# First stage of a two-layer trunk step: shift and scale from stationary weights, with the first query and key products made inside the stage

## The chip, the cores and the metric

The kernel runs on one core of a Trainium2 chip. A core has five engines that work side by side and meet through semaphores: TensorE (PE in the profile; its weight loads are listed as PEld), VectorE (DVE), ScalarE (ACT), GpSimd (POOL) and SyncE (SP). SP, ACT and POOL can issue DMAs, which run on 16 shared DMA engines. The metric is the time of one execution on the device in microseconds (us), the median of several runs.

## The reference

The reference is one inference step through two layers. 640 tokens of width 1024 go through it: 512 latent tokens on a grid and 128 context tokens. Layer 0 is neighbourhood attention with 16 heads, layer 1 a recurrent unit; after each comes a SwiGLU block. What matters here is the very beginning: the first normalization with its shift and scale, and the first query and key products.

```python
def _adaln(cond, w_mod, b_mod):
    m = jax.nn.silu(cond) @ w_mod + b_mod
    return jnp.split(m, N_MOD, axis=-1)

def _modulate(x, g, shift, scale):
    return _rms_norm(x, g) * (1 + scale[:, None, :]) + shift[:, None, :]

sh1_c, sc1_c, ... = _adaln(c_ctx[None, :], w_mod[i], b_mod[i])
sh1_l, sc1_l, ... = _adaln(c, w_mod[i], b_mod[i])
xm_c = _modulate(ctx, norm_g[i, 0], sh1_c, sc1_c)
xm_l = _modulate(lat, norm_g[i, 0], sh1_l, sc1_l)
q, k, v = jnp.split(xm @ w_qkv, 3, axis=-1)
```

There are two conditioning vectors (latent and context), so the shift and the scale of the first sub-layer are a product of a 2x1024 matrix with a 1024x2048 weight: 8 MB of weights for two rows of result.

## The kernel before

Activations lie with features on the 128 partitions and tokens along the free dimension: x is 8 feature tiles of 128x640. Every large product is made in three parts. Weights and activations are split into a high part of a reduced type (fp32r) and the rest, and hi x hi, hi x lo and lo x hi are added up in PSUM. The three products are lines 221, 222 and 223 (method `some`), for two chunks of 320 tokens each. One unit of 128 output features is thus 8 feature tiles x 3 products x 2 chunks = 48 products. `unit` (line 163) loads a unit's weights into `raw`, copies them to `whi` on ACT (line 180) and subtracts to get `wlo` on DVE (line 182); each of the three tags has 3 buffers.

The first stage is `start` (line 296). It works in this order:

1. The eight tiles of x are loaded on SP; each is squared on ACT and added to `ssq` on DVE (lines 315 to 319).
2. The shift and scale products come in four rounds of two feature tiles. The conditioning vectors, padded to 32 columns (`csp`), are the stationary side, and 256 columns of w_mod move (line 342). Four of the eight input tiles sit side by side in the array, so each result arrives in four parts on four groups of 32 partitions. The w_mod pieces come in 16 DMAs of 512 KB into 10 buffers (`sw`, `wb`).
3. The results are copied out of PSUM to a row (lines 353 and 354). A second product with a selection matrix `sel` adds the four parts and turns them so that features lie on partitions (line 357). Lines 363 and 364 make A (scale) and B (shift).
4. In the first round, `stat` turns the sum of squares into 1/rms for all tokens, spread over all partitions (lines 396 to 413, copied by line 347). POOL multiplies the odd feature tiles of x with it (line 350).
5. `scaled` applies A and B of the round before: the even tiles through `modulate` (lines 418 to 420), the odd ones on ACT (line 325) and `split` (lines 1076 and 1077). The results are the tiles `hi` and `lo` that all Q, K and V products read.

After `start`, `qk` (line 529) makes Q and K of the first head pair, 48 products each, `vq` the V columns of four heads (lines 236 to 238), and the loop over eight head pairs runs `attend(p)` and `qk(p + 1)`. The products of one pair fill PE while the softmax of another runs on DVE and ACT. `fill` puts one step of the other modulations (one POOL DMA `mraw` and two DVE products, line 250) behind a softmax.

The order of the instructions on each engine is mostly the planner's: it takes them in the order of the code, but lets later ones go first where an earlier one would wait by its own estimate. `tc.issue_after(ins)` pins an instruction behind another. That is why in the trace the first Q products stand between the shift and scale products.

[...] Buffers of a tag are taken in turn; `bufs` is their number.

## Time and profile before

| | |
|---|---|
| median of 3 runs | 1532.3 us (1531.98 to 1537.51) |
| span of the profiled execution | 1532.6 us |
| PE busy | 1483.2 us (97%) |
| DVE busy | 1062.8 us (69%) |
| ACT busy | 695.8 us (45%) |
| POOL busy | 256.1 us (17%) |
| bytes moved by DMA | 196.65 MB, 128 GB/s on average |
| first product of w_mod (line 342) | starts at 12.83 us |
| first Q product (line 221) | starts at 28.84 us |
| first V product (line 236) | starts at 57.64 us |

The profile is one execution on the chip. Its own time is the span, 0.3 us above the median. A timeline row reads: start and length in us, engine, line and operation, output <- inputs, shapes, count; in brackets the idle time before it and what ended it. A row with a count covers all instructions from the first start to the last end. A row of stretches reads: from:to, length, busy time of PE, weight loads, DVE, ACT and POOL with counts, then the clock granted to TensorE (1.00 is full), the share of time that the DMA engines are busy, and GB/s. Busy times of PE include pipelined ends, so the distance between the starts of two neighbouring rows is the cost of a product, not its length.

### The profile page before, as it was taken

What the parts mean: (1) busy time and instruction counts of PE and PEld (TensorE: products, weight loads), DVE (VectorE), ACT (ScalarE), POOL (GpSimd) and SP (SyncE); (2) the same over time, 40 slices, a digit from 0 to 9 for tenths busy, and PEclk for the clock granted to TensorE, in tenths of its full rate; (3) what the DMA queues carried; (4) which work ended last, traced back from release to release, by engine and by line L of the source; (5) the groups of instructions that cost most, each with busy time, mean ns of one, the idle gap of its engine ahead of it and who ended that gap; (6) DMA issues with size and microseconds to landing.
All of it is one profiled execution on the core that took longest, in us unless ns stands there. A gap on an engine that the chain in (4) does not pass through costs nothing.

```text
span 1532.6 us, 25990 instructions
## 1 busy us (share of the span) xinstructions
PE 1483.2 (97%) x10309; PEld 1438.5 (94%) x10309; DVE 1062.8 (69%) x2000; ACT 695.8 (45%) x1266; POOL 256.1 (17%) x270
## 2 busy tenths in 40 slices
PE   5999999989999999999999999999899999999997
PEld 4899999879999999999999988799899999999996
DVE  5668888969899888434443869885965656566556
ACT  5566767755333113312331478863534342424242
POOL 2101122100111110000000113230412323222210
PEclk8999999999999999999999999999999999999999
DMA  9545656445566664222223443334332231323221
GB/s 375 155 115 166 185 158 179 147 141 184 177 194 191 192 201 140 73 83 71 76 61 99 153 127 107 107 104 162 113 119 70 83 110 56 99 67 97 70 56 69
DMA packets 73098, 196.65 MB, mean 128 GB/s; under 512 B 8048, under 2 KB 25616, under 8 KB 72848
## 3 DMA queue, kind: packets, MB, share of 16 engines
q1 hardware_dynamic: 58832, 144.48, 30.0%
q0 software_dynamic: 13856, 50.35, 10.8%
q8 instruction: 81, 1.33, 0.4%
q14 instruction: 41, 0.34, 0.1%
q10 hardware_dynamic: 288, 0.16, 0.0%
HBM read 179.48 MB, written 8.92 MB: 123 GB/s over the span
## 4 chain that ended last, share of the span: by engine, by line
PE 85%; DVE 7%; ACT 4%; DMA 2%; issue 2%; SPq 0%; POOL 0%; POOLq 0%; DVEq 0%; ACTq 0%
PE mm L222 14%; PE mm L223 14%; PE mm L221 14%; PE mx L221 5%; PE mx L223 5%; PE mx L222 5%; PE mx L850 3%; PE mx L849 3%; PE mx L851 3%; PE op L687 2%; PE gp L1035 2%; PE tp L611 2%; PE mc L849 1%; PE mc L850 1%; PE mc L851 1%
## 5 line engine op out<-in xcount | busy, mean ns | idle before, releaser
L222 PE MATMUL mm<-big,whi 128*128 128x320 f32 (+3 forms) x1270 | 397.9, 314 | 3.0 <-DVE big L1077 2.1
L221 PE MATMUL mm<-big,whi 128*128 128x320 f32 (+3 forms) x1270 | 394.5, 313 | 3.7 <-ACT big L1076 2.3
L223 PE MATMUL mm<-big,wlo 128*128 128x320 f32 (+3 forms) x1270 | 396.8, 313 | 1.0 <-DVE wlo L182 1.0
L222 PEld LDWEIGHTS mm<-big,whi 128*128 128x128 f32 x1270 | 241.9, 190 | 6.6 <-DVE big L1077 4.4
L221 PEld LDWEIGHTS mm<-big,whi 128*128 128x128 f32 x1270 | 240.3, 190 | 7.5 <-ACT big L1076 2.8
L223 PEld LDWEIGHTS mm<-big,wlo 128*128 128x128 f32 x1270 | 241.5, 190 | 2.5 <-DVE wlo L182 1.4
L250 DVE SCALAR_TENSOR_TENSOR mprod<-mraw,csb 128x1024 f32<-128x1024 f32 x160 | 195.4, 1221 | 11.2 <-DMA mraw<-in_wm 10.7
L443 DVE SCALAR_TENSOR_TENSOR x<-mm,G,x 128x128 f32<-128x128 f32 (+3 forms) x205 | 83.5, 436 | 86.6 <-PE mm L223 86.6
L182 DVE TENSOR_TENSOR wlo<-raw,whi 128x1024 fp32r<-128x1024 f32 (+1 forms) x90 | 110.1, 1224 | 37.4 <-ACT whi L180 22.1
L180 ACT CAST whi<-raw 128x1024 fp32r<-128x1024 f32 (+1 forms) x74 | 76.8, 1037 | 110.1 <-PE mm L222 71.7
L221 PE MATMUL mm<-big,whx 128*128 128x320 f32 (+3 forms) x363 | 113.7, 313 | 0.0
L223 PE MATMUL mm<-big,wlx 128*128 128x320 f32 (+3 forms) x363 | 113.3, 312 | 0.0
L222 PE MATMUL mm<-big,whx 128*128 128x320 f32 (+3 forms) x363 | 113.1, 312 | 0.0
L246 POOL DMA_DIRECT2D mraw<-in_wm x80 | 43.3, 542 | 381.1 <-DVE mprod L250 264.9
L221 PE MATMUL mx<-big,whi 128*128 128x320 f32 (+3 forms) x298 | 93.5, 314 | 0.4 <-ACT big L1076 0.4
L223 PE MATMUL mx<-big,wlo 128*128 128x320 f32 (+3 forms) x298 | 93.0, 312 | 0.0
L222 PE MATMUL mx<-big,whi 128*128 128x320 f32 (+3 forms) x298 | 92.9, 312 | 0.0
L180 ACT CAST whx<-raw 128x1024 fp32r<-128x1024 f32 (+1 forms) x40 | 41.0, 1027 | 93.4 <-PE mm L222 54.2
L221 PE MATMUL mx<-big,whx 128*128 128x320 f32 (+3 forms) x245 | 75.6, 309 | 0.0
L223 PE MATMUL mx<-big,wlx 128*128 128x320 f32 (+3 forms) x245 | 75.5, 308 | 0.0
L1076 ACT CAST whi<-raw 128x1024 fp32r<-128x1024 f32 (+1 forms) x41 | 41.3, 1008 | 74.8 <-PE mm L222 45.0
L222 PE MATMUL mx<-big,whx 128*128 128x320 f32 (+3 forms) x245 | 75.2, 307 | 0.0
(301 smaller groups left out, 3620.8 us busy)
## 6 DMA issues: line engine op xcount, KB each, us to landing
raw<-in_gu SPq DMA_DIRECT2D x88, 512.0 KB, 3.6
mraw<-in_wm POOLq DMA_DIRECT2D x80, 512.0 KB, 4.0
raw<-in_dn SPq DMA_DIRECT2D x24, 512.0 KB, 3.7
raw<-in_wqk SPq DMA_DIRECT2D x16, 512.0 KB, 4.4
raw<-in_wi SPq DMA_DIRECT2D x16, 512.0 KB, 3.6
whi<-in_wi POOLq DMA_DIRECT2D x16, 512.0 KB, 4.0
raw<-in_dn SPq DMA_DIRECT2D x16, 448.0 KB, 3.4
sw<-in_wm SPq DMA_DIRECT2D x10, 512.0 KB, 10.5
```

The source lines that it names most:

```text
L180: nc.scalar.copy(hi, raw)
L182: nc.vector.tensor_tensor(lo, raw, hi.bitcast(F32), ALU.subtract)
L221: nc.tensor.matmul(ps, hi[:, k], xhi[:, k, s], start=(k == 0), stop=False)
L222: nc.tensor.matmul(ps, hi[:, k], xlo[:, k, s], start=False, stop=False)
L223: nc.tensor.matmul(ps, lo[:, k], xhi[:, k, s], start=False, stop=(k == last))
L246: nc.gpsimd.dma_start(w, self.i["wm"][l * 6 + j - 2, f])
L250: nc.vector.scalar_tensor_tensor(prod, w, 1.0, self.csb[:, s], ALU.mult, ALU.mult, accum_out=out[:, s, f:f + 1])
L443: self.nc.vector.scalar_tensor_tensor(xs, ps[:, a - t0:b - t0], G[:, s, f:f + 1], xs, ALU.mult, ALU.add)
L849: nc.tensor.matmul(ps, hi[:, k], xh[:, k], start=start and k == 0, stop=False, skip_group_check=not start)
L850: nc.tensor.matmul(ps, hi[:, k], xl[:, k], start=False, stop=False, skip_group_check=not start)
L851: nc.tensor.matmul(ps, lo[:, k], xh[:, k], start=False, stop=(k == KH - 1), skip_group_check=not start)
L1076: self.nc.scalar.copy(hi, v)
```

## The change

- **w_mod** is laid out anew: 16 pieces of 512 KB, one for each feature tile k and each of shift (j = 0) and scale (j = 1). Each piece has its own buffer (`sw{k}{j}`). Requests on SP stand in a fixed order: x, pieces of tile 0, weights of the first Q, pieces of tile 1, weights of the first K and second Q, then the pieces of tiles 2 to 7.
- **vectors(k)**: w_mod is now the stationary side. For each j and each of the 8 input tiles c, a 128x128 block of the piece is loaded and multiplied with the two conditioning columns. A and B come straight from PSUM (`coefficients`); the copies, the selection product and the products on POOL are gone.
- **Scaling**: x is multiplied with 1/rms on DVE (`normed`), ACT writes the high part (`high`), DVE the scaled x and the low part (`low`).
- **Products**: Q of pair 0, K of pair 0 and Q of pair 1 are made inside `start`, in six PSUM banks that stay open, feature tile by feature tile. The vectors of tile k + 1 stand ahead of the products of tile k. Their evictions are split off from `qk` (`queries`, `keys_tile`).
- **Order**: `order` pins every PE, DVE and ACT instruction of the stage behind the one before it on its engine.
- **Dummy products**: before the sum of squares is ready, PE multiplies the identity with itself six times and with each arriving tile of x.
- **Around it**: tag `r` has 2 buffers, K moves to the main pool, the activation of the spread conditioning vectors is pinned behind the last Q eviction, the DMA scratch is set to 4096.

```diff
-        "wm0": wm[0, :, :2 * D].reshape(2, 4, P, 2, 4, 256).transpose(3, 4, 0, 2, 1, 5),
+        "wm0": wm[0, :, :2 * D].reshape(KT, P, 2, KT, P).transpose(3, 2, 1, 0, 4),
...
     def start(self, hi, lo, sp, big):
         nc = self.nc
         b1 = self.t([P, KT], F32, "b1", 1, sp)
         nc.vector.tensor_scalar(b1, self.col("bsc"), 1.0, None, ALU.add)
         idle = big.rearrange("p k t -> p (k t)")
+        cond = self.cs.rearrange("p (s k) -> p k s", s=2)
+        last = {}
+
+        def order(engine, step, after=None):
+            with ExitStack() as st:
+                for ins in (last.get(engine), after):
+                    if ins is not None:
+                        st.enter_context(self.tc.issue_after(ins))
+                last[engine] = step().ins
+            return last[engine]
+
+        def pe(*args, **kw):
+            return order("PE", lambda: nc.tensor.matmul(*args, **kw))
+
+        def dve(op, *args, **kw):
+            return order("DVE", lambda: op(*args, **kw))
+
+        def act(*args, **kw):
+            return order("ACT", lambda: nc.scalar.activation(*args, **kw))
+
+        for k in range(KT):
             nc.sync.dma_start(self.x[:, k], self.i["x"][k * P:k * P + P])
+        pieces, us = {}, []
+
+        def request(k):
+            for j in range(2):
+                pieces[k, j] = self.t([P, KT, P], F32, f"sw{k}{j}", 1, sp)
+                nc.sync.dma_start(pieces[k, j], self.i["wm0"][k, j])
+
+        def weights(f):
+            raw, whi_, wlo_ = [self.t([P, KT, P], dt, v, 3) for dt, v in ((F32, "raw"), (F32R, "whi"), (F32R, "wlo"))]
+            nc.sync.dma_start(raw, self.i["wqk"][f])
+            us.append((whi_, wlo_, raw))
+        request(0)
+        weights(0)
+        request(1)
+        weights(KT)
+        weights(1)
+        for k in range(2, KT):
+            request(k)
+
+        aux = self.ps("at")
+        for _ in range(6):
+            pe(aux[:, 0:P], self.ident, self.ident, start=True, stop=True)
+        self.ssq = self.t([P, NTOK], F32, "ssq", 2, sp)
+        for k in range(KT):
+            pe(aux[:, 0:256], self.ident, self.x[:, k, 0:256], start=True, stop=True)
+            q = self.ssq if k == 0 else idle[:, 2048 + k % 4 * NTOK:2688 + k % 4 * NTOK]
+            act(q, self.x[:, k], AF.Square)
+            if k:
+                dve(nc.vector.tensor_tensor, self.ssq, self.ssq, q, ALU.add)
+
+        def vectors(k):
+            pm = self.ps("ss")
+            for j in range(2):
+                for c in range(KT):
+                    pe(pm[:, 2 * j:2 * j + 2], pieces[k, j][:, c], cond[:, c], start=(c == 0), stop=(c == KT - 1))
+            return pm
+
+        def coefficients(k, pm):
+            B, A = [self.t([P, 2], F32, v, 3, sp) for v in ("b0", "a0")]
+            dve(nc.vector.tensor_scalar, A, pm[:, 2:4], b1[:, k:k + 1], self.col("ng00", k), ALU.add, ALU.mult)
+            dve(nc.vector.tensor_scalar, B, pm[:, 0:2], self.col("bsh", k), None, ALU.add)
+            return A, B
+
+        blocks = range(0, NTOK, P)
+        for j, b in enumerate(blocks):
+            pe(aux[:, 256 + j:257 + j], self.ssq[:, b:b + P], self.ones[:, 0:1], start=True, stop=True)
+        v = self.t([P, 8], F32, "var", 2)[:, 0:NT]
+        dve(nc.vector.tensor_scalar, v, aux[:, 256:256 + NT], 1.0 / D, EPS, ALU.mult, ALU.add)
+        rs = self.t([P, 8], F32, "rs", 2)[:, 0:NT]
+        nc.gpsimd.tensor_tensor(rs, v, self.mhalf.broadcast_to([P, NT]), ALU.pow)
+        dg = self.t([P, NT, P], F32, "dg", 1, sp)
+        dve(nc.vector.tensor_tensor, dg, self.ident.unsqueeze(1).broadcast_to([P, NT, P]), rs.unsqueeze(2).broadcast_to([P, NT, P]), ALU.mult)
+        pm = vectors(0)
+        rr = [self.ps("kk") for _ in range(2)]
+        for j, b in enumerate(blocks):
+            pe(rr[j // 4][:, b % NLAT:b % NLAT + P], self.ones, dg[:, j], start=True, stop=True)
+
+        def whi(j):
+            hi_, lo_, raw = us[j]
+            act(hi_, raw, AF.Copy)
+
+        def wlo(j):
+            hi_, lo_, raw = us[j]
+            dve(nc.vector.tensor_tensor, lo_, raw, hi_.bitcast(F32), ALU.subtract)
+
+        def normed(k):
             for s, a, b in _pieces(0, NTOK):
                 v = self.x[:, k, a:b]
+                dve(nc.vector.tensor_tensor, v, v, r[:, a:b] if k else rr[s][:, 0:b - a], ALU.mult)
+
+        def high(k, A, B):
+            for s, a, b in _pieces(0, NTOK):
+                act(hi[:, k, a:b], self.x[:, k, a:b], AF.Identity, scale=A[:, s:s + 1], bias=B[:, s:s + 1])
+
+        def low(k, A, B):
+            for s, a, b in _pieces(0, NTOK):
+                v = self.x[:, k, a:b]
+                dve(nc.vector.tensor_scalar, v, v, A[:, s:s + 1], B[:, s:s + 1], ALU.mult, ALU.add)
+            dve(nc.vector.tensor_tensor, lo[:, k, 0:NTOK], self.x[:, k, 0:NTOK], hi[:, k, 0:NTOK].bitcast(F32), ALU.subtract)
+
+        def products(k, kind, tiles=range(3)):
+            for j in tiles:
+                w, m = us[j][kind == "lh"], (lo if kind == "hl" else hi)
+                for c, (t0, t1) in enumerate(CH):
+                    pe(pss[2 * j + c], w[:, k], m[:, k, t0:t1], start=(kind == "hh" and k == 0), stop=(kind == "lh" and k == KT - 1))
+
+        r = self.t([P, NTOK], F32, "ssq", 2, sp)
+        AB = {0: coefficients(0, pm)}
+        normed(0)
+        whi(0)
+        high(0, *AB[0])
+        for j, (_, t0, t1) in enumerate(_pieces(0, NTOK)):
+            act(r[:, t0:t1], rr[j][:, 0:t1 - t0], AF.Copy)
+        pss = [self.pg(False)[:, 0:HT]]
+        pss += [self.ps("kk")[:, 0:HT]]
+        low(0, *AB[0])
+        normed(1)
+        products(0, "hh", (0,))
+        pm = vectors(1)
+        products(0, "hl", (0,))
+        wlo(0)
+        AB[1] = coefficients(1, pm)
+        whi(1)
+        high(1, *AB[1])
+        whi(2)
+        low(1, *AB[1])
+        pss += [(self.ps("kk") if j % 2 else self.pg(False))[:, 0:HT] for j in range(4)]
+        products(0, "hh", (1,))
+        products(0, "hl", (1,))
+        products(0, "lh", (0,))
+        products(1, "hh", (0, 1))
+        products(0, "hh", (2,))
+        products(0, "hl", (2,))
+        products(1, "hh", (2,))
+        products(1, "hl")
+        wlo(1)
+        wlo(2)
+        normed(2)
+        pm = vectors(2)
+        products(0, "lh", (1, 2))
+        products(1, "lh")
+        AB[2] = coefficients(2, pm)
+        high(2, *AB[2])
+        low(2, *AB[2])
+        for k in range(2, KT):
+            if k + 1 < KT:
+                normed(k + 1)
+                pm = vectors(k + 1)
+                AB[k + 1] = coefficients(k + 1, pm)
+                high(k + 1, *AB[k + 1])
+                low(k + 1, *AB[k + 1])
+            for kind in ("hh", "hl", "lh"):
+                products(k, kind)
+        made = [self.queries(), self.keys_tile(), self.queries()]
+        for j in range(6):
+            t0, t1 = CH[j % 2]
+            made[j // 2][1](t0, slice(t0, t1), pss[j])
+        return [m[0] for m in made]
...
-    def qk(self, p, hi, lo, ap):
-        nc = self.nc
-        Q = self.t([P, NTOK], F32, "r", 1)
+    def queries(self):
+        nc = self.nc
+        Q = self.t([P, NTOK], F32, "r", 2)
...
-                nc.scalar.mul(Q[:, NLAT:NTOK], ps[:, 192:320], 0.125)
+                self.opened = nc.scalar.mul(Q[:, NLAT:NTOK], ps[:, 192:320], 0.125).ins
+        return Q, eq
+
+    def keys_tile(self):
+        nc = self.nc
+        K = self.t([P, 960], F32, "K", 1)
...
-        self.ws(self.i["wqk"][p], hi, lo, eq, 0)
-        self.ws(self.i["wqk"][KT + p], hi, lo, ek, 0)
+        return K, ek
+
+    def qk(self, p, hi, lo, ap, Q=None, K=None):
+        nc = self.nc
+        if Q is None:
+            Q, eq = self.queries()
+            self.ws(self.i["wqk"][p], hi, lo, eq, 0)
+        if K is None:
+            K, ek = self.keys_tile()
+            self.ws(self.i["wqk"][KT + p], hi, lo, ek, 0)
...
-        with self.phase("start", at=2, rr=1, sc=1, sh=1) as sp:
+        with self.phase("start", at=1, ss=1, kk=3) as sp:
...
-            self.start(xhi, xlo, sp, wbig)
+            Q, K, Q1 = self.start(xhi, xlo, sp, wbig)
...
-            QK = self.qk(0, xhi, xlo, ap)
+            QK = self.qk(0, xhi, xlo, ap, Q, K)
             self.vq(0, xhi, xlo, V)
             nc.sync.dma_start(self.csb, bass.AP(tensor=i["cc"].tensor, offset=0, ap=[[0, P], [1, 2 * D]]))
-            nc.scalar.activation(self.csb, self.csb, AF.Silu)
+            with self.pin(self.opened):
+                nc.scalar.activation(self.csb, self.csb, AF.Silu)
...
-                    QK = self.qk(p + 1, xhi, xlo, ap)
+                    QK = self.qk(p + 1, xhi, xlo, ap, None if p else Q1)
...
-    nc = _bacc.Bacc("TRN2", target_bir_lowering=False, num_devices=1)
+    nc = _bacc.Bacc("TRN2", target_bir_lowering=False, num_devices=1, dynamic_dma_scratch_size=4096)
```

The lines of the old `start` that the new one replaces stand in the kernel above and are left out of the diff, as are the same changes of `bufs` for tag `r` in two other methods.

More of the change, by code (lines that the diff above doesn't have):

```diff
@@ L38 @@
 MODS = ((0, 2), (0, 4), (0, 3), (0, 5), (1, 1), (1, 0), (1, 4), (1, 3), (1, 2), (1, 5))
-NB = 2
 KH = KT // 2
@@ L297, in start @@
         nc = self.nc
-        csp = self.t([P, KT, 32], F32, "csp", 1, sp)
-        nc.gpsimd.memset(csp, 0.0)
-        nc.scalar.copy(csp[:, :, 0:2], self.cs.rearrange("p (s k) -> p k s", s=2))
-        sel = self.t([P, 2], F32, "sel", 1, sp)
-        nc.vector.tensor_reduce(sel, self.ident.rearrange("p (g c) -> p c g", g=4)[:, 0:2], AX.X, ALU.add)
         b1 = self.t([P, KT], F32, "b1", 1, sp)
@@ L305, in start @@
         idle = big.rearrange("p k t -> p (k t)")
-        big = self.t([P, 5120], F32, "wb", 1, sp)
-        free = [big[:, j * D:j * D + D] for j in range(5)]
-        free = [self.t([P, D], F32, f"sw{j}", 1, sp) for j in range(5)] + free
-        use = 0
-        def load_x(k):
-            nc.sync.dma_start(self.x[:, k], self.i["x"][k * P:k * P + P])
-            if k == 0:
-                self.ssq = self.t([P, NTOK], F32, "ssq", 2, self.sb)
-                nc.scalar.activation(self.ssq, self.x[:, k], AF.Square)
-                return
-            q = idle[:, 2048 + k % 4 * NTOK:2688 + k % 4 * NTOK]
-            nc.scalar.activation(q, self.x[:, k], AF.Square)
-            nc.vector.tensor_tensor(self.ssq, self.ssq, q, ALU.add)
@@ L321, in scaled @@
-        def scaled(k, A, B):
+        cond = self.cs.rearrange("p (s k) -> p k s", s=2)
[9 more added lines that the diff above has]
+            return order("PE", lambda: nc.tensor.matmul(*args, **kw))
@@ L322, in scaled @@
+        rr = [self.ps("kk") for _ in range(2)]
[8 more added lines that the diff above has]
+        def normed(k):
             for s, a, b in _pieces(0, NTOK):
                 v = self.x[:, k, a:b]
-                if k % 2:
-                    nc.scalar.activation(v, v, AF.Identity, scale=A[:, s:s + 1], bias=B[:, s:s + 1])
-                else:
-                    self.modulate(k, a, b, A[:, s:s + 1], B[:, s:s + 1], v, hi, lo)
@@ L328, in scaled @@
-            if k % 2:
-                self.split(hi[:, k, 0:NTOK], lo[:, k, 0:NTOK], self.x[:, k, 0:NTOK])
-        for k in range(KT):
-            load_x(k)
-        todo, ro, n = [], 0, NB * P
-        for k0 in range(0, KT, NB):
-            pm = [self.ps("sh"), self.ps("sc")]
-            for h in range(2):
-                for j in range(2):
-                    w = free[use % len(free)][:, 0:4 * n].rearrange("p (k n) -> p k n", k=4)
-                    use += 1
-                    nc.sync.dma_start(w, self.i["wm0"][j, k0 // NB, h])
-                    for k4 in range(4):
-                        nc.tensor.matmul(pm[j][32 * k4:32 * k4 + 32, 0:n], csp[:, 4 * h + k4], w[:, k4], start=(h == 0), stop=(h == 1))
-            if k0 == 0:
-                rsb = self.t([P, NTOK], F32, "ssq", 2, self.sb)
-                for _, t0, t1 in _pieces(0, NTOK):
-                    self.stat(t0, t1)
-                    nc.scalar.copy(rsb[:, t0:t1], self.r[0][:, 0:t1 - t0])
-                self.r = rsb, 0
-                for k in range(1, KT, 2):
-                    nc.gpsimd.tensor_tensor(self.x[:, k], self.x[:, k], rsb, ALU.mult)
-            row = idle[:, ro:ro + 2 * n]
-            ro += 2 * n
-            nc.vector.tensor_copy(row[:, 0:n], pm[0][:, 0:n])
-            nc.scalar.copy(row[:, n:2 * n], pm[1][:, 0:n])
-            pt = self.ps()
-            for q in range(2 * NB):
-                nc.tensor.matmul(pt[:, 2 * q:2 * q + 2], row[:, q * P:q * P + P], sel, start=True, stop=True)
-            new = []
-            for kb in range(NB):
-                k = k0 + kb
-                A = self.t([P, 2], F32, "a0", 4, sp)
-                B = self.t([P, 2], F32, "b0", 4, sp)
-                nc.vector.tensor_scalar(A, pt[:, 2 * (NB + kb):2 * (NB + kb) + 2], b1[:, k:k + 1], self.col("ng00", k), ALU.add, ALU.mult)
-                nc.vector.tensor_scalar(B, pt[:, 2 * kb:2 * kb + 2], self.col("bsh", k), None, ALU.add)
-                new.append((k, A, B))
-            for t in todo:
-                scaled(*t)
-            todo = new
@@ L369, in start @@
-        for t in todo:
-            scaled(*t)
+                dve(nc.vector.tensor_tensor, v, v, r[:, a:b] if k else rr[s][:, 0:b - a], ALU.mult)
[7 more added lines that the diff above has]
+            dve(nc.vector.tensor_tensor, lo[:, k, 0:NTOK], self.x[:, k, 0:NTOK], hi[:, k, 0:NTOK].bitcast(F32), ALU.subtract)
@@ L433, in stats @@
     def stats(self):
-        rt = self.t([P, NTOK], F32, "r", 1)
+        rt = self.t([P, NTOK], F32, "r", 2)
         for t0, t1 in CH[::-1]:
@@ L535, in cr @@
             return v.rearrange("p (c r) -> p c r", r=ROWS)
-        K = self.t([P, 960], F32, "K", 1, ap)
         def eq(t0, s, ps):
@@ L797, in project_halves @@
             out(f, *CH[0], self.chunk(us[f], hi, lo, *CH[0]))
-        self.rt = self.t([P, NTOK], F32, "r", 1)
+        self.rt = self.t([P, NTOK], F32, "r", 2)
         for c, (t0, t1) in enumerate(CH):
```

## The prediction

> **What bounds the kernel now.** I read the page first: the engines' busy time, then the slices.

> ```profile
> span 1532.6 us, 25990 instructions
> PE 1483.2 (97%) x10309; PEld 1438.5 (94%) x10309; DVE 1062.8 (69%) x2000; ACT 695.8 (45%) x1266; POOL 256.1 (17%) x270
> ...
> PE   5999999989999999999999999999899999999997
> ...
> PEclk8999999999999999999999999999999999999999
> DMA  9545656445566664222223443334332231323221
> ```

> TensorE (PE) has work 97% of the time. The exception is the first slice, where PE is half busy, the clock is not always full and the DMA engines are at their limit: the stage that the change rewrites. Next, busy time by stretches:

> ```profile
> 10.00:15.00 5.00, 2.17 (x14) 1.40 (x14) 3.13 (x4) 2.05 (x3) 0.00 (x0) 1.00 1.03 413
> ...
> 35.00:40.00 5.00, 5.00 (x36) 3.48 (x35) 1.90 (x4) 1.19 (x3) 0.00 (x0) 0.81 1.03 409
> ...
> 12.80:57.60 44.80, 39.71 (x276) 30.09 (x277) 26.21 (x52) 20.21 (x37) 14.43 (x16) 0.85 0.81 308
> ...
> 57.60:290.00 232.40, 232.40 (x1905) 222.90 (x1904) 186.46 (x468) 157.08 (x332) 36.56 (x60) 1.00 0.54 159
> ```

> The columns are stretch, length, busy time of PE, weight loads, DVE, ACT, POOL, then granted clock, DMA share, GB/s. From 57.6 to 290 us PE never idles at full clock. So what counts is one point: when PE has finished a given set of products. Earlier means a shorter kernel, later a longer one.

> ```profile
> 52.13 0.47 PE L221 MATMUL mm<-big,whi 128*128 128x320 f32 x1
> ...
> 53.47 0.47 PE L221 MATMUL mm<-big,whi 128*128 128x320 f32 x1
> ...
> 54.56 0.31 PE L221 MATMUL mm<-big,whi 128*128 128x320 f32 x1
> ...
> 57.20 0.31 PE L221 MATMUL mm<-big,whi 128*128 128x320 f32 x1
> ...
> 57.64 0.28 PE L236 MATMUL mm<-whi,big 128*128 128x256 f32 x1
> ...
> L221 PE MATMUL mm<-big,whi x32: 304/354/637, 28.8 to 57.2; 128*128 128x320 f32 x32
> ```

> Line 221 is one of three kinds of products (221, 222, 223); 32 of each, 96 in all, make the first Q and K. They are over when the first V product starts, at 57.6. At full clock the rows at 54.56 and 57.20 are 18 products apart: 0.147 us each. At half clock (52.13 to 53.47, five products) it is 0.268. The changed first stage makes Q, K and also the second Q: 48 products more. Before therefore stands at 57.6 + 48 x 0.147 = 64.6 us in the same units.

> **The change: the weight loads.** Now w_mod is stationary: per feature tile 16 products in the code, 128x128 weights against 2 columns, in fp32. Line 357 is that shape, with 16 products in the code; line 396 has one column.

> ```profile
> L357 PE MATMUL at<-sel,big x32: 165/251/376, 20.2 to 45.2; 128*128 128x2 f32 x32
> ...
> 13.84 2.21 PEld L396 LDWEIGHTS at<-ones,ssq 128*128 128x128 f32 x10 [0.81 <-DVE ssq L319]
> ...
> L396 PEld LDWEIGHTS at<-ones,ssq x54: 186/192/338, 13.8 to 1522.0; 128*128 128x128 f32 x54
> ...
> 40.08 0.56 PEld L357 LDWEIGHTS at<-sel,big 128*128 128x128 f32 x4
> ...
> 383.45 0.30 PEld L399 LDWEIGHTS at<-ones,sq 128*128 128x128 f32 x2
> ...
> 384.35 0.30 PEld L399 LDWEIGHTS at<-ones,sq 128*128 128x128 f32 x2
> ```

> 16 in the code are 32 in the trace: fp32 takes two passes, each with its own load. So the change has 8 x 16 x 2 = 256 loads. Eight of them lie between 383.45 and 384.35: 0.1125 us each, and 40.08 agrees. The columns are nothing, the load is all. At 13.84 ten take 2.21 with 0.34 for the last (the longest in the view of that line): (2.21 - 0.34) / 9 = 0.21 us. So 256 loads are 28.8 us at full and 53.8 us at half clock.

> **The change: the rest of the stage.**

> ```profile
> 8.90 4.54 DVE L319 TENSOR_TENSOR ssq<-ssq,big 128x640 f32<-128x640 f32 x5 [0.25 <-ACT big L318]
> ...
> L319 DVE TENSOR_TENSOR ssq<-ssq,big 128x640 f32<-128x640 f32 x7 | 5.8, 826 | 4.5 <-ACT big L318 4.0
> ...
> L418 DVE SCALAR_TENSOR_TENSOR big<-big,a,ssq 128x512 f32<-128x512 f32 x4 | 3.4, 850 | 0.0
> ...
> L419 ACT ACTIVATE big<-big,b 128x512 fp32r<-128x512 f32 x4 | 2.9, 713 | 2.3 <-DVE big L418 2.3
> ...
> L180 ACT CAST whi<-raw 128x1024 fp32r<-128x1024 f32 x7 | 7.3, 1047 | 1.7 <-PE mm L238 1.1 <-PE mm L222 0.6
> ...
> L182 DVE TENSOR_TENSOR wlo<-raw,whi 128x1024 fp32r<-128x1024 f32 x7 | 9.7, 1387 | 3.1 <-ACT whi L180 3.1
> ...
> L543 ACT ACTIVATE r<-mm 128x128 f32<-128x128 f32 x4 | 0.9, 274 | 3.2 <-DVE r L541 3.2
> ...
> L413 PE MATMUL rr<-dg,ones 128*128 128x128 f32 x10 | 2.1, 357 | 0.0
> ```

> Start: the sum of squares is ready at 8.90 + 4.54 = 13.4 us; its ten loads and the ten of line 413 follow, 1.1 us each group warm, 2.1 cold. PE then waits for the first normalized tile (850 + 713 ns and handoffs, some 1.8 us) and for the second tile's coefficients and scaling (1.2): 3.0 us.
> Dummy products before 13.4 fill idle time: nothing.
> Transfers: behind x, 16 pieces and 3 weight tiles of 0.52 MB are 10 MB; at 413 GB/s, counted from 11 us, the last lands near 35 us, well before its turn below: hidden. A tile lands in 2.6 us while PE spends 6.2 on it, so the fixed request order costs nothing. The V weights wait on SP for raw buffers, with the large condition tile, cached keys and bias tables behind them; all are used after the stage: hidden.
> DVE spends some 3.1 us per tile (two passes like L319, a scaling of under 850 ns and small ones), ACT 1.1: hidden behind 6.2 us of PE. The removed work (the products of lines 342 and 357, the copies of their rows, the products on POOL) is credited already, since I count up to an absolute point.

> Warm sum: 13.4 + 1.1 + 1.1 + 28.8 + 144 x 0.147 = 21.2 + 3.0 = **68.6 us**, against 64.6 before. Half-clock sum: 13.4 + 2.1 + 2.1 + 53.8 + 38.6 + 3.0 = 113.0.

> **The clock between them.**

> ```profile
> 13.80:16.05 2.25, 2.25 (x14) 2.21 (x10) 0.16 (x1) 0.00 (x0) 0.06 (x1) 1.00 1.02 410
> ...
> 26.00:27.00 1.00, 0.11 (x1) 0.11 (x1) 0.53 (x2) 0.82 (x3) 1.00 (x1) 0.81 1.08 434
> ...
> 36.00:37.00 1.00, 1.00 (x10) 0.22 (x9) 0.74 (x1) 0.00 (x0) 0.00 (x0) 0.57 1.06 422
> ...
> 50.00:51.00 1.00, 0.71 (x3) 0.72 (x4) 0.87 (x2) 0.00 (x0) 1.00 (x2) 0.76 0.99 160
> ...
> 53.00:54.00 1.00, 1.00 (x6) 1.00 (x5) 0.23 (x1) 0.42 (x1) 0.00 (x0) 0.53 1.03 408
> ...
> 47.10:50.50 3.40, 1.98 (x10) 1.49 (x11) 2.90 (x5) 2.05 (x5) 3.33 (x7) 1.00 0.46 116
> 50.50:53.90 3.40, 3.40 (x14) 3.40 (x14) 0.82 (x3) 0.87 (x3) 1.44 (x3) 0.50 0.97 319
> ...
> 1078.00:1081.30 3.30, 2.83 (x23) 2.75 (x22) 3.30 (x3) 1.65 (x2) 0.00 (x0) 1.00 0.37 70
> ```

> From the shares of the clock, it fell at 26.62, rose at 36.86, fell at 50.52, rose at 53.94: multiples of 3.41 us apart. The stretch ahead of the fall at 50.5 held 10 products, 1.5 us of 3.4; the one ahead of the rise was full. So the clock is decided on a grid of 3.4 us by the work of the last stretch. Does a load with 2 columns count as work? From 13.8 to 16.05 PE issued ten such loads without a gap and still ran slow (the listed 1.00 is no record of a raise: 0.21 per load is the half rate). Against it, 1078 to 1081.3 mixes products and 12 loads and no fall follows. I take it that loads count little. A streak of 32 takes 3.6 us; with 2.6 us of products behind it some stretch per tile is mostly loads, the clock falls for one 3.4 us stretch, and 1.7 us of work is lost. Eight tiles: 8 x 1.7 = 13.6, the end is 68.6 + 13.6 = **82.2 us**. Two lost stretches per tile give 95.8, none 68.6.

> [...]

> **The change: after the stage.**

> ```profile
> mraw<-in_wm POOLq DMA_DIRECT2D x80, 512.0 KB, 4.0
> ```

> V's weights need the buffers of the three first units, free only as the last products finish: at most one cast and one subtraction (1047 + 1387 ns) behind some 2.4 us of evictions on ACT (nine like L543), 4.8 us; at least nothing, since the buffers come free up to 12 products (1.8 us) early. I take 2, nearest to the cast and subtraction alone. With the second Q made early, attention lacks 48 products that could fill PE's waits in its first round: 0 to 7.0 us; I take 1, as DVE has room (186 of 232 us). The condition tile's activation moves behind the last Q eviction, needed a round later: 0. [...] More buffers and K's other pool: 0, their only effect is earlier issue.

> Sum: 82.2 - 64.6 + 2 + 1 = +20.6 on the span of 1532.6 (median of the runs 1532.3): **1553 us**.

> **Rivals.** (1) The loads keep the clock up: 68.6 - 64.6 + 3 = +7.0, 1539.6, within 0.5% (7.7 us), about what a measurement can tell from no change. For it: 1078 to 1081.3. Against: 13.8 to 16.05. (2) Faster: a load with a short product costs less than I read.

> ```profile
> 91.83 1.90 PE op L687 x32
> ```

> Here 32 loads with half-wide weights take 59 ns each. At that price 256 are 15.1 us, the end is 54.9 even warm, -9.7 + 3 = -6.7: 1526. It decides below (64.6 - 3 - 39.8) / 256 = 85 ns. Against it: lines 357 and 399 have the exact shape at 112. [...] (3) The clock stays low nearly throughout: 113.0 - 64.6 + 3 = +51, 1584. Products of 18 in a row, as at 50.5 to 53.9, speak against it.

> **How the numbers follow.** Forecast 0.68, rival 1 0.20, rival 2 0.07, rival 3 0.05. Forecast and rival 3 are slower by over 0.5%, with a little of rival 1 (its V wait at the upper end): 0.75. Within 0.5%: 0.17. Faster: rival 2 and a hundredth of rival 1: 0.08. The range reaches from 1536 (rival 1 with nothing lost behind the stage: 68.6 - 64.6 = +4) to 1567 (two low stretches per tile: 95.8 - 64.6 + 3 = +34). The forecast's own range is 1544 to 1567.

> **What would show it.** Right: 256 loads of the new line 0.11 us apart where the clock is full and 0.21 where it is half; granted clock well below 1 between 15 and 80 us, in steps of 3.4 us; the first V product between 75 and 96 us; PE idle only a few us between. Wrong: first V product before 65 us, loads under 85 ns apart, or a PE that waits for pieces of w_mod (then transfers bound the stage and my sum is beside the point). The V start at 68 to 70 with full clock is rival 1. A gain or loss that appears after 330 us would be none of this.

## The result and the profile after

The changed kernel takes 1567.3 us (median of four runs, 1562.8 to 1573.5) against 1532.4 us of the kernel before on the same chip: a ratio of 1.0231 (95% interval 1.021 to 1.0252), 34.9 us slower. That is in the direction of the forecast, but 14.3 us above its 1553 and 0.3 us above the upper end of its range. The profiled execution has a span of 1562.4 us, 29.8 us more than the profiled execution before.

The page of the changed kernel: engines, then PE's slices, the granted clock and the DMA slices.

```profile
span 1562.4 us, 26205 instructions
PE 1525.2 (98%) x10433; PEld 1484.4 (95%) x10433; DVE 1064.6 (68%) x2013; ACT 692.0 (44%) x1257; POOL 247.2 (16%) x264
...
PE   8999999989999999999999999999999999999997
...
PEclk7689999999999999999999999999999999999998
DMA  9144555544556666222222343325242322222211
```

PE is busy in the first slice now, but the clock row begins with 7, 6 and 8 where before it began with 8 and then 9s. The DMA row shows the transfers done early: 9, then 1. The loss lies in the first three slices of 39 us.

The timeline of PE in the changed kernel (start, length, operation, operands, count, and in brackets the wait):

```profile
13.14 1.28 PE L312 MATMUL at<-ones,ssq 128*128 128x1 f32 x10 [1.35 <-DVE ssq L315]
14.28 6.64 PE L312 MATMUL ss<-cs,sw 128*128 128x2 f32 x32
...
24.45 0.64 PE L312 MATMUL mm<-big,whi 128*128 128x320 f32 x1 [1.20 <-ACT big L318]
...
25.27 6.82 PE L312 MATMUL ss<-cs,sw 128*128 128x2 f32 x32
...
37.00 3.63 PE L312 MATMUL ss<-cs,sw 128*128 128x2 f32 x32
40.49 0.40 PE L312 MATMUL mm<-big,wlo 128*128 128x320 f32 x1
...
41.91 0.43 PE L312 MATMUL kk<-big,wlo 128*128 128x320 f32 x1
42.14 6.83 PE L312 MATMUL ss<-cs,sw 128*128 128x2 f32 x32
...
53.07 4.50 PE L312 MATMUL ss<-cs,sw 128*128 128x2 f32 x32
...
89.79 0.31 PE L312 MATMUL kk<-big,wlo 128*128 128x320 f32 x1
92.52 0.39 PE L235 MATMUL mm<-whi,big 128*128 128x256 f32 x1 [2.43 <-ACT r L630]
```

Each streak of 32 loads takes 3.63 us or 6.8 us, 0.11 or 0.21 us a load, and some lie between, where the clock changed inside. The last product of the stage starts at 89.79; the first V product follows at 92.52 after a wait of 2.43 us for the evictions. The kernel before stood at 64.6 us in the same units.

The same time in stretches, cut where the granted clock changes. The columns are those of the prediction's stretches: the number behind the counts of POOL is the clock.

```profile
14.64:35.12 20.48, 19.28 (x86) 18.89 (x87) 7.75 (x17) 5.99 (x9) 1.19 (x1) 0.50 1.03 412
35.12:41.95 6.83, 6.83 (x56) 6.83 (x55) 3.45 (x6) 0.84 (x2) 0.00 (x0) 1.00 0.84 342
41.95:52.19 10.24, 10.24 (x47) 10.24 (x47) 4.70 (x11) 1.56 (x3) 0.00 (x0) 0.50 0.01 3
52.19:55.60 3.41, 3.41 (x31) 3.41 (x30) 0.57 (x2) 0.00 (x0) 0.00 (x0) 1.00 0.00 0
55.60:62.43 6.83, 6.83 (x29) 6.83 (x30) 2.83 (x7) 1.20 (x2) 0.00 (x0) 0.50 0.25 77
62.43:65.84 3.41, 3.41 (x33) 3.41 (x32) 0.00 (x0) 0.00 (x0) 0.00 (x0) 1.00 0.04 11
65.84:69.25 3.41, 3.41 (x14) 3.41 (x14) 2.20 (x6) 1.20 (x2) 0.00 (x0) 0.50 0.54 146
69.25:72.67 3.42, 3.42 (x31) 3.42 (x30) 0.64 (x2) 0.00 (x0) 0.00 (x0) 1.00 0.02 5
72.67:79.50 6.83, 6.83 (x29) 6.83 (x29) 2.84 (x7) 1.20 (x2) 0.00 (x0) 0.50 0.00 0
79.50:82.91 3.41, 3.41 (x33) 3.41 (x32) 0.00 (x0) 0.00 (x0) 0.00 (x0) 1.00 0.00 0
82.91:86.32 3.41, 3.41 (x15) 3.41 (x15) 2.13 (x5) 1.20 (x2) 2.61 (x5) 0.50 0.00 0
...
93.15:96.56 3.41, 3.41 (x18) 3.41 (x18) 2.91 (x10) 2.84 (x6) 0.00 (x0) 0.50 0.97 359
96.56:290.00 193.44, 191.73 (x1561) 182.94 (x1561) 153.59 (x393) 132.84 (x277) 29.51 (x50) 1.00 0.53 156
```

All the lengths are multiples of 3.41 us. A stretch at full clock with 31 to 33 instructions of PE is wholly or mostly a streak of loads (the two with 31 hold about 24 loads behind the last products of a tile), and a half-clock stretch follows every such one. The fall at 41.95 came behind less than that: the 3.41 us before it hold 17 loads and the ten products from 40.49 to 41.91. PE has no gap in those from 35.12 to 86.32 (10.24 busy of 10.24, at a clock of 0.50). Between 14 us and the first V product lie 6 + 3 + 2 + 1 + 2 + 1 = 15 half-clock stretches, where the prediction had 8; one more falls into the V products, behind the wait of 2.43 us.

### The profile page after: what moved, and what is told of

Read it like the earlier page. It is cut to its first block, busy times and chain, and to the rows that moved or that the text cites. A ratio compares the mean times of both kernels' runs of the same rounds, so it can differ in the third digit from the quotient of the medians.

```text
span 1562.4 us, 26205 instructions
## 1 busy us (share of the span) xinstructions
PE 1525.2 (98%) x10433; PEld 1484.4 (95%) x10433; DVE 1064.6 (68%) x2013; ACT 692.0 (44%) x1257; POOL 247.2 (16%) x264
## 4 chain that ended last, share of the span: by engine, by line
PE 85%; DVE 7%; ACT 5%; DMA 2%; issue 2%; SPq 0%; POOL 0%; POOLq 0%; DVEq 0%; ACTq 0%
PE mm L221 13%; PE mm L222 13%; PE mm L220 13%; PE mx L220 5%; PE mx L222 5%; PE mx L221 5%; PE mx L949 3%; PE mx L950 3%; PE mx L951 3%; PE ss L312 2%; PE op L787 2%; PE tp L711 1%; PE gp L1135 1%; PE mc L949 1%; PE mc L951 1%
## 5 line engine op out<-in xcount | busy, mean ns | idle before, releaser
L220 PE MATMUL mm<-big,whi 128*128 128x320 f32 (+3 forms) x1233 | 383.3, 312 | 3.1 <-ACT big L1176 2.7
L221 PE MATMUL mm<-big,whi 128*128 128x320 f32 (+3 forms) x1233 | 383.9, 312 | 2.2 <-DVE big L1177 2.1
L222 PE MATMUL mm<-big,wlo 128*128 128x320 f32 (+3 forms) x1233 | 384.2, 312 | 0.0
L220 PEld LDWEIGHTS mm<-big,whi 128*128 128x128 f32 x1233 | 232.5, 189 | 5.6 <-ACT big L1176 3.5
L221 PEld LDWEIGHTS mm<-big,whi 128*128 128x128 f32 x1233 | 233.2, 189 | 4.7 <-DVE big L1177 3.4
L222 PEld LDWEIGHTS mm<-big,wlo 128*128 128x128 f32 x1233 | 233.1, 189 | 1.1
L181 DVE TENSOR_TENSOR wlo<-raw,whi 128x1024 fp32r<-128x1024 f32 (+1 forms) x87 | 105.4, 1213 | 31.8 <-ACT whi L179 20.6
L179 ACT CAST whi<-raw 128x1024 fp32r<-128x1024 f32 (+1 forms) x71 | 73.5, 1037 | 112.7 <-PE mm L221 68.3
L220 PE MATMUL mm<-big,whx 128*128 128x320 f32 (+3 forms) x356 | 110.6, 311 | 0.0
L222 PE MATMUL mm<-big,wlx 128*128 128x320 f32 (+3 forms) x356 | 110.2, 310 | 0.0
L221 PE MATMUL mm<-big,whx 128*128 128x320 f32 (+3 forms) x356 | 110.0, 309 | 0.0
L220 PE MATMUL mx<-big,whi 128*128 128x320 f32 (+3 forms) x287 | 90.1, 314 | 0.2 <-ACT whi L179 0.2
L222 PE MATMUL mx<-big,wlo 128*128 128x320 f32 (+3 forms) x287 | 89.3, 311 | 0.0
L221 PE MATMUL mx<-big,whi 128*128 128x320 f32 (+3 forms) x287 | 89.3, 311 | 0.0
L220 PE MATMUL mx<-big,whx 128*128 128x320 f32 (+3 forms) x252 | 78.3, 311 | 0.0
L221 PE MATMUL mx<-big,whx 128*128 128x320 f32 (+3 forms) x252 | 78.2, 310 | 0.0
L222 PE MATMUL mx<-big,wlx 128*128 128x320 f32 (+3 forms) x252 | 78.1, 310 | 0.0
L1176 ACT CAST whi<-raw 128x1024 fp32r<-128x1024 f32 (+1 forms) x41 | 41.4, 1009 | 73.6 <-PE mm L221 45.3
## 6 DMA issues: line engine op xcount, KB each, us to landing
raw<-in_gu SPq DMA_DIRECT2D x88, 512.0 KB, 3.5
mraw<-in_wm POOLq DMA_DIRECT2D x80, 512.0 KB, 3.8
raw<-in_dn SPq DMA_DIRECT2D x24, 512.0 KB, 3.7
sw<-in_wm SPq DMA_DIRECT2D x16, 512.0 KB, 10.1
raw<-in_wqk SPq DMA_DIRECT2D x16, 512.0 KB, 4.2
raw<-in_wi SPq DMA_DIRECT2D x16, 512.0 KB, 3.5
whi<-in_wi POOLq DMA_DIRECT2D x16, 512.0 KB, 4.2
```

The costliest lines, as they stand in the source:

```text
L179: nc.scalar.copy(hi, raw)
L181: nc.vector.tensor_tensor(lo, raw, hi.bitcast(F32), ALU.subtract)
L220: nc.tensor.matmul(ps, hi[:, k], xhi[:, k, s], start=(k == 0), stop=False)
L221: nc.tensor.matmul(ps, hi[:, k], xlo[:, k, s], start=False, stop=False)
L222: nc.tensor.matmul(ps, lo[:, k], xhi[:, k, s], start=False, stop=(k == last))
L1176: self.nc.scalar.copy(hi, v)
```

## The experiments

The theory: TensorE that only loads weights and lets 2 columns pass does not count as working, so the clock falls at the end of each 3.41 us stretch filled with loads, and comes back only behind a stretch full of products. The rivals: the loads lower the clock or cost their time as such, whatever passes behind them; and the loss lies in other parts of the change (the fixed order, the late V weights, the filler, the DMA scratch).

**More columns behind the same loads.** Three runs repeat the two conditioning columns. The first has 96 columns:

```diff
+        wide = self.t([P, KT, 96], F32, "wide", 1, sp)
+        nc.vector.tensor_copy(wide.rearrange("p k (r s) -> p k r s", s=2), cond.unsqueeze(2).broadcast_to([P, KT, 48, 2]))
...
-  pe(pm[:, 2 * j:2 * j + 2], pieces[k, j][:, c], cond[:, c], ...)
+  pe(pm[:, 96 * j:96 * j + 96], pieces[k, j][:, c], wide[:, c], ...)
```

> The changed kernel, in which each of the 256 loads of shift and scale weights is followed by 96 columns instead of 2 (the two conditioning columns repeated 48 times; the same sums, the same loads in the same order). Theory A (the granted clock falls because streams of loads with 2 columns don't count as work): the clock stays at 1 from the first load stream on, apart from at most two stretches of 3.4 us; a load stream of 32 takes 3.6 to 4.8 us everywhere, the first V product comes between 70 and 80 us instead of at 92.5, and the whole kernel takes 1545 to 1553 us although it streams 48 times as many columns in these products. Theory B (it is the price of the loads as such, or their heavy use, that lowers the clock): the clock is half in about 15 stretches of the stage as in the changed kernel, and the time is 1567 us or, by the longer streams, more.

Measured: 1542.7 us (1540.9 to 1548.9), ratio to before 1.0062 (1.004 to 1.0084): 2.3 us below the range expected. Two stretches and two rows of PE's timeline of this run:

```profile
15.10:18.51 3.41, 3.41 (x18) 3.41 (x18) 0.90 (x2) 1.06 (x1) 1.19 (x1) 0.50 1.02 414
18.52:74.46 55.94, 50.73 (x394) 49.09 (x392) 30.68 (x63) 15.97 (x28) 6.28 (x10) 1.00 0.53 203
...
31.71 3.71 PE L314 MATMUL ss<-wide,sw 128*128 128x96 f32 x32
...
74.46 0.39 PE L235 MATMUL mm<-whi,big 128*128 128x256 f32 x1 [2.44 <-ACT r L632]
```

From 14 us on one half-clock stretch is left, at 15.10; from 18.52 on the clock is full. A streak takes 3.71 us, as long as the streaks with 2 columns at full clock: 48 times the columns cost nothing there, and the kernel is 24.6 us faster for them. The rival that blames the loads for the clock falls, and so does every explanation by which much work lowers the clock.

Then 32 and 64 columns, with the same edit and other numbers:

> The changed kernel with 32 columns behind each load instead of 2 (against 96 before, which kept the clock up). Theory A (share of columns): a third of the share that the 96 columns gave, so load streams alone stay under the point of the fall; the clock falls in the streams as with 2 columns, and the time is 1560 to 1572 us. Theory C (any width above a few columns counts as work): the clock is as with 96 columns and the time about 1540.

> The changed kernel with 64 columns behind each load: between the 32 that let the clock fall in pure load streams and the 96 that held it. By the share: two thirds of the 96 columns' share, about 0.47 of a stretch when a product of this type is counted twice per column, just above the 0.4 where it fell elsewhere: the clock stays full from about 30 us on, and the time is 1537 to 1548 us. If it falls in the streams as with 32 columns, the bound lies higher than I read it, and the time is 1550 to 1562 us.

Measured: 1560.1 us with 32 (1556.3 to 1567.7; ratio 1.0185, 1.0152 to 1.0218) and 1548.8 us with 64 (1540.6 to 1551.2; ratio 1.0091, 1.0062 to 1.012). First two stretches with 32 columns, then two streaks and two stretches with 64:

```profile
42.26:45.68 3.42, 3.42 (x34) 3.42 (x32) 2.43 (x5) 0.42 (x2) 0.00 (x0) 1.00 0.03 6
45.68:49.09 3.41, 3.41 (x15) 3.41 (x15) 1.84 (x5) 1.20 (x2) 0.00 (x0) 0.50 0.14 38
```

```profile
25.59 6.92 PE L314 MATMUL ss<-wide,sw 128*128 128x64 f32 x32
...
42.44 3.68 PE L314 MATMUL ss<-wide,sw 128*128 128x64 f32 x32
...
15.07:35.55 20.48, 19.28 (x86) 18.88 (x86) 7.77 (x17) 5.99 (x9) 1.19 (x1) 0.50 1.03 412
35.55:79.93 44.38, 41.19 (x323) 40.65 (x322) 23.57 (x48) 10.87 (x20) 6.27 (x10) 1.00 0.29 99
```

With 32 columns a streak at full clock (34 instructions from 42.26) still takes the clock down. With 64 it does not: once up at 35.55, the clock is full until 79.93, past the end of the stage. But 64 columns did not bring it up: the streak at 25.59 ran 6.92 us at half clock, two stretches long, and the clock stayed half until 35.55, where the same streak at 42.44 held a full clock. That need not be a second bound, since a streak at half clock also passes half as many columns in 3.41 us. Some 16 loads fit into such a stretch and some 30 at full clock: 16 x 64 = 1024 columns did not raise the clock and 16 x 96 = 1536 did, 30 x 32 = 960 let it fall and 30 x 64 = 1920 held it. One bound between 1024 and 1536 columns of this kind fits all four. As the clock came up late, the time is 0.8 us above what I expected. The four widths in one table (half-clock stretches counted in the record of the granted clock from 14 us to the first V product):

| columns behind each load | half-clock stretches | first V product, us | time, us |
|---|---|---|---|
| 2 (the change) | 15 | 92.52 | 1567.3 |
| 32 | 12 | 88.14 | 1560.1 |
| 64 | 6 | 80.10 | 1548.8 |
| 96 | 1 | 74.46 | 1542.7 |

From 2 to 96 columns, 14 stretches fewer bring the V product 18.1 us forward: 1.3 us each, against the 1.7 of the prediction.

**The same instructions in another order.** From the third tile on, products of tile k stand between the loads for tile k + 1:

```diff
 for c in range(KT):
     pe(pm[:, 2 * j:2 * j + 2], pieces[k, j][:, c], cond[:, c], ...)
+    between(j * KT + c)      # 18 products of the tile before, spread over loads 4 to 15
```

> The changed kernel, in which from the third feature tile on the 18 query and key products of a tile stand between the load products of the next tile instead of behind all of them: the same instructions on TensorE in another order. Theory A (a stretch of the 3.41 us grid that is filled by loads alone makes the clock fall): no stretch holds loads alone any more, each holds 18 products of 320 columns to 32 loads, so that there are fewer half-clock stretches between 37 us and the first V product than the 9 of the changed kernel; each one saved is worth about 1.7 us, so 1552 to 1564 us. As the mixture has columns in only some 2.65 of 6.25 us, it may sit near the point of the fall, and a clock that stays half throughout the mixture is the miss that is possible, at about 1570 us. Theory B (the order within a tile doesn't matter): within 0.3% of the changed kernel's 1567 us.

Measured: 1578.7 us (1572.6 to 1581.9), ratio 1.028 (1.0243 to 1.0317): slower than the changed kernel, the miss that the text calls possible, though 9 us above the 1570 that it names. Two stretches of this run:

```profile
38.09:48.33 10.24, 10.24 (x84) 10.24 (x84) 4.96 (x11) 1.20 (x2) 0.00 (x0) 1.00 0.37 124
48.33:106.35 58.02, 56.83 (x237) 55.29 (x237) 15.01 (x35) 8.04 (x13) 6.28 (x10) 0.50 0.10 32
```

The clock fell at 48.33, behind the stretch in which the mixture begins (with ten loads alone; that stretch held 17 loads and ten products in all), and then stayed at half for 58 us, 17 stretches: none held loads alone, but only the last was nearly full of products. Six extra products per tile should have lifted the mixture over the point of the fall:

```diff
+ if n % 2:
+     pe(aux[:, 0:HT], us[0][0][:, 0], hi[:, 0, 0:HT], start=True, stop=True)
```

> The spread order of the run before last, with six more products of 320 columns per feature tile in the mixture (results of no use, into a scratch bank): 36 more products, 5.3 us at the full clock. Theory A (the share of the time in which columns pass decides the clock, and the spread order lay just under what keeps it up): the share rises from about 0.39 to about 0.45, the clock stays full in the mixture once it is up at about 40 us, and the time falls from 1579 to 1550 to 1560 us although the work grows. Theory B (the order or the number of weight loads decides, not the columns): the clock stays half as in the spread order and the time rises by 5 to 10 us to about 1587.

Measured: 1587.5 us (1582.3 to 1590.8), ratio 1.0355 (1.0328 to 1.0382). The extra products are 30 in the trace, not 36. Read alone, the time speaks for the rival. The stretches say that it was no test of it:

```profile
38.35:41.76 3.41, 3.41 (x32) 3.41 (x31) 0.23 (x2) 0.00 (x0) 0.00 (x0) 1.00 0.79 297
41.76:118.00 76.24, 75.31 (x313) 74.28 (x313) 18.12 (x42) 9.52 (x15) 6.26 (x10) 0.50 0.09 26
```

The third tile's loads, which this edit left in a streak of their own, filled the stretch from 38.35 and took the clock down before the mixture began; in it, it never came back. The next run removes that streak, puts products ahead of the mixture and thickens it to 28 products for 32 loads:

```diff
- pm = vectors(2)
+ pm = vectors(2, lambda n: extra(1 + n % 2))
...
+ extra(18)
...
+ if n < 4 or n % 2:
+     extra(1)
```

> The spread order once more, because in its run with six extra products the third tile's loads, which still stood alone, took the clock down just before the mixture, and at the half clock the mixture's share of columns never rose above 0.63. Now the third tile's loads have extra products between them too (24), 18 stand in front of the mixture, and each tile of it has 10: 92 extra products in all, 13.5 us at the full clock. Theory A (the clock falls below a share of about 0.4 of a 3.41 us stretch and comes back only above about 0.8, so what counts is to come into the mixture at the full clock): the clock stays full from about 40 us to the first V product, apart from two stretches, and the time is 1553 to 1566 us, well below the 1579 and 1587 us of the spread runs with less work. Theory B (the number of weight loads in the mixture holds the clock down whatever stands before it): half clock as before, and about 1597 us.

Measured: 1567.7 us (1565.9 to 1572.1), ratio 1.0228 (1.0196 to 1.026).

```profile
14.65:38.55 23.90, 22.70 (x101) 22.30 (x101) 9.48 (x19) 5.99 (x9) 1.19 (x1) 0.50 1.02 411
38.55:93.16 54.61, 53.08 (x398) 51.49 (x397) 18.18 (x43) 7.21 (x12) 2.98 (x5) 1.00 0.14 42
```

The clock was full for 54.6 us through the whole mixture with the same 32 loads per tile. 92 products of no use make the kernel 11.0 us faster than the spread order without them (9.4 us, when each is taken against the kernel before on its own chip), and 19.8 us faster than with only some of them. The time is 1.7 us above my range. What that comes from is not shown; the start holds seven half-clock stretches from 14.65 to 38.55, one more than in the change.

**Few loads.** Seven of the eight input tiles are left out of the shift and scale products.

```diff
-                for c in range(KT):
+                for c in range(1):
```

> The changed kernel with only one of the eight input tiles taken into the shift and scale products: seven eighths of this product of the computation are left out, 32 loads instead of 256. Everything else of the change stands (own buffers, fixed order, one tile ahead, no row copy and no turning product). Theory A (the loads and the clock that they cost are the whole loss): the stage is bound by the last pieces, which land at about 41 us, and its first V product comes between 45 and 52 us, against 57.6 before and 92.5 in the changed kernel; the time is 1512 to 1526 us. Theory B (part of the loss lies in the V weights that come late, the filler that is left, or the fixed order): slower than the kernel before, above 1535 us.

Measured: 1525.3 us (1523.5 to 1528.4), ratio 0.9942 (0.9923 to 0.9961). The time is in the range, the place is not:

```profile
53.50 0.41 PE L312 MATMUL mm<-big,whi 128*128 128x320 f32 x1 [1.28 <-DVE big L315]
...
57.97 0.54 PE L235 MATMUL mm<-whi,big 128*128 128x256 f32 x1 [2.41 <-ACT r L630]
```

The first V product comes at 57.97, not at 45 to 52: with the loads gone DVE's work per tile is next in line (1.28 us of waiting at 53.50), not the transfers (in the changed kernel the last piece of w_mod lands at 36.05, not at about 41). Still, the kernel is faster than before with everything else of the change in it, the wait behind the stage too (2.41 us). So the loads and their clock are more than the whole net loss.

**The other direction of the product.** Everything of the change but the stationary weights: w_mod moves against 32 conditioning columns as before, and the last tile's products go unit by unit.

```diff
-  pe(pm[:, 2 * j:2 * j + 2], pieces[k, j][:, c], cond[:, c], ...)
+  g = c % 4 * 32
+  pe(pm[g:g + 32, j * P:j * P + P], csp[:, c], pieces[k, j][:, c], start=(c < 4), stop=(c >= 4))
...
+  act(row, pm[:, 0:2 * P], AF.Copy)
...
+  pe(pm[:, 256 + 2 * j:258 + 2 * j], row[:, j * P:j * P + P], sel, start=True, stop=True)
```

> The changed kernel's order, buffers and one tile ahead, but with the shift and scale weights moving again as in the kernel before (32 columns stationary, four column groups, copy of the row by ScalarE, two small products that turn it), and with the last tile's products unit by unit. Theory A (of the change's two halves, the order is worth something and the stationary weights lose it): no streams of loads, the first V product between 45 and 56 us, the time 1512 to 1530 us, below the kernel before. Theory B (the fixed order is itself a loss, since the turning stands in front of products that could run): 1535 us or more.

Measured: 1525.4 us (1524.8 to 1527.0), ratio 0.9941 (0.992 to 0.9962): 9.4 us faster than before and 42 us faster than the change. PE's timeline and one stretch:

```profile
50.60 1.08 PE L316 MATMUL ss<-sw,csp 128*32 128x128 f32 x32
...
57.74 0.41 PE L316 MATMUL mm<-big,whi 128*128 128x320 f32 x1 [2.41 <-DVE big L319]
...
60.23 0.28 PE L235 MATMUL mm<-whi,big 128*128 128x256 f32 x1
...
22.04:60.23 38.19, 34.00 (x380) 29.65 (x369) 27.26 (x57) 15.75 (x31) 6.26 (x10) 1.00 0.67 253
```

A tile's shift and scale products take 1.08 us here instead of 3.6 to 6.8, and the clock is full from 22.04 on. The V product comes 4 us later than I expected, since PE waits 2.41 us for DVE ahead of the last tile. Placing the turning product earlier, by one group of six products (a third of a tile, not half), should have cut that wait:

```diff
 half = vectors(k + 1)
-products(k, "hh")
+products(k - 1, "lh")
 pm = turned(*half)
```

> The version with moving weights, fixed order and one tile ahead, in which the turning product of the next tile is put half a tile earlier (behind the third group of products of the tile before), so that VectorE's and ScalarE's chain for the last tile starts earlier. Theory: the wait of 2.4 us for VectorE before the last tile's products shrinks by 1 to 2 us, and the time goes from 1525.4 to 1522 to 1525 us. Rival: VectorE is slowed there by GpSimd's memory work at 53.6 us whatever the order, and the time stays.

Measured: 1525.9 us (1522.3 to 1527.9), ratio 0.9949 (0.993 to 0.9968): the same, and 0.9 us above the range expected.

```profile
25.48:32.31 6.83, 6.55 (x38) 5.48 (x42) 4.93 (x9) 2.15 (x3) 0.00 (x0) 0.50 1.03 410
...
59.10 0.42 PE L316 MATMUL mm<-big,whi 128*128 128x320 f32 x1 [1.58 <-DVE big L319]
...
61.59 0.28 PE L235 MATMUL mm<-whi,big 128*128 128x256 f32 x1
```

The wait fell from 2.41 to 1.58 us, but the last tile starts 1.4 us later: in this execution the clock was half from 25.48 to 32.31 us too, the stretch shown first. A gain of under 1 us is lost in that. The rival there, a VectorE slowed by GpSimd whatever the order, has one row of the run with moving weights for it (DVE's scaling from 54.51 takes 1.91 us where the tile before took 0.81, beside two MEMSETs on POOL from 53.60 to 55.44); it is not tested by this: the time stayed, but the wait did not.

**The DMA scratch alone**, on the kernel before:

```diff
-    nc = _bacc.Bacc("TRN2", target_bir_lowering=False, num_devices=1)
+    nc = _bacc.Bacc("TRN2", target_bir_lowering=False, num_devices=1, dynamic_dma_scratch_size=4096)
```

> The kernel before with one line of the change alone: the scratch of the dynamic DMA queue set to 4096. All theories here put this at nothing: within 0.3% of the kernel before, 1530 to 1538 us. If it moved the time, part of what was put on the loads would belong here.

Measured: 1532.2 us, ratio 0.9998 (0.9982 to 1.0014): nothing, as expected.

## Why the prediction came out too low, and which step failed

- **The point that counts.** Right: 89.94 (the last product's start and 0.147) less 64.6 is 25.3 us; the wait up to 92.52 adds 2.6, the half-clock stretch in the V products 1.5, and 193.44 - 191.73 = 1.7 us of idle PE follow before 290 us. Together 31.1, against 29.8 us between the two spans.
- **Start, loads, transfers.** The sum of squares is taken up at 13.14 (13.4); loads cost 0.11 and 0.21 us; PE never waits for a piece of w_mod, and the last one lands at 36.05 (35). All that was right. The 3.0 us of waits at the start are 1.20 in the trace, 1.8 too many.
- **The warm sum.** Nearly right: in the run with 96 columns the stage ends near 74.46 - 2.44 = 72.0; less one half-clock stretch it is 70.5, against 68.6.
- **The clock: this step failed.** The prediction took one lost stretch of 3.4 us per tile, 8 x 1.7 = 13.6. The direction and the grid are what the runs show, but 15 stretches were lost, nearly two per tile. Three things were missing. After a fall, the tile's 18 products at half clock are only 18 x 0.268 = 4.8 us of work between streaks; when the grid cuts them so that no stretch is full of products, the second one stays at half too (55.60 to 62.43, 72.67 to 79.50). A streak that begins at half clock is itself nearly twice as long (6.83 us from 42.14, against 3.63 from 37.00) and fills two stretches (41.95 to 48.77). And in the first two tiles loads, normalization and waits follow each other with hardly a product, so the clock was half for six stretches in a row. The prediction had two per tile (95.8) as the end of its range only.
- **What a stretch costs.** The 1.7 takes half clock for half speed. By the prediction's own rows a product takes 0.268 instead of 0.147 us and a load 0.21 instead of 0.1125, so a stretch loses 1.5 to 1.6 us. At 1.55, 15 of them are 23 us instead of 13.6, and the prediction's sum becomes 68.6 - 1.8 + 23.2 = 90.0, against the measured 89.94. The 1.3 from the comparison with 96 columns is lower in part because that run waits longer within the stage: 55.94 - 50.73 - 2.44 = 2.8 us, against 1.2.
- **Behind the stage.** The V weights: 2 predicted, 2.43 measured, but the agreement is luck. The wait ended with an eviction on ACT that freed a PSUM buffer at 92.5, and that eviction stood behind three weight casts (88.70 to 91.64); the prediction counted one cast and one subtraction behind the evictions. The filler: 1 predicted, 1.7 us of idle time measured up to 290 us, of which 1.60 is one wait for a DMA into KS at 202 us; that the missing 48 products would have filled it is not shown. That the wait ahead of V itself costs a half-clock stretch (93.15 to 96.56, another 1.5 us) was not in the sum.
- **The other executions.** The median lies 3.2 us above the profiled execution's own time (1564.2). The four runs have mean clocks of 0.977, 0.974, 0.972 and 0.968 in the order of their times. That the grid falls differently on the streaks each time would explain it, and the forecast took one profile's worth of it. Where the grid starts was not varied, so this stays a reading of four runs.
- **Rivals.** The loads do not keep the clock up (rival 1): the row from 41.95 is busy without a gap at 0.50. No load came under 85 ns (rival 2): 32 of them take 3.63 us at full clock. Products between the streaks bring the clock back (rival 3): behind those from 48.82 the row from 52.19 is at 1.00 again.

**Where the clock falls and where it rises.** The traces kept hold more on this than the single runs. I added up the columns that passed in each 3.41 us stretch between 13 and 125 us of all twelve traces, a product that a boundary cuts counted in part. In 302 of these 392 stretches at most 60 of the columns are behind fp32 loads, so nearly all belong to the large products. Seven of them, each with its run and the start of the stretch:

| clock in the stretch | half behind it | full behind it |
|---|---|---|
| full | 3036 columns (before, 47.11); 2932 (the change, 38.53) | 3200 (spread order, 41.50); 2936 (spread order, 38.09) |
| half | 2955 (spread order with 30 extra products, 113.44) | 3460 (spread order, 102.94); 3664 (the change, 31.71) |

What stays open: the exact factor between the two kinds of columns; and why the version with moving weights gains 7.4 us on the span while its V product gains only 64.6 - 60.2 = 4.4.

## What to carry to other kernels

Count columns, not instructions: in these runs a product with few columns cost its weight load (32 took 3.63 us with 2 columns behind each and 3.71 with 96), and where such loads with 2 columns filled a stretch of 3.41 us, the next one ran at half clock. So here the thin operand belongs on the stationary side (1.08 us a tile against 3.6 to 6.8). Where a mixture of loads and products was unavoidable, what mattered was to enter it at full clock and to let enough columns pass: 3200 in 3.41 us held the clock, 3036 did not. A profile that shows PE busy at 98% says nothing of that; the granted clock beside it (0.50 in 15 stretches from 14 us to the first V product) does.

## What was not expected of the hardware

- TensorE was issuing without a gap and was still granted half the clock: with 2 columns behind each load and also with 32 (10.24 us busy of 10.24 from 41.95 and 3.41 of 3.41 from 45.68, both at 0.50).
- More work saved time: 48 times the columns behind the loads took 24.6 us off, and 92 products of no use some 10 us.
- The same instructions held a full clock and failed to bring it back: a streak of loads with 64 columns did both (3.68 us from 42.44 at full clock, 6.92 us from 25.59 at half). Counted in columns that pass in 3.41 us, the fall and the rise lie at about the same point (3036 and 2955 columns were too few, 3200 and 3460 enough), but at half clock only about half as many pass (0.268 us a product against 0.147).
